# Soft mixture of experts on one core: operand products of two experts moved ahead of the first expert's products, and ScalarE's copies moved ahead of its casts

## The chip, the cores and the metric

The kernel runs on one core of a Trainium2 chip. The metric is the device time of one execution in microseconds (us). TensorE (PE in the profile) multiplies matrices and writes to PSUM; VectorE (DVE) and ScalarE (ACT) do elementwise work and copy results out of PSUM; GpSimd (POOL) and SyncE (SP) mostly issue transfers here. Each engine works through its own list of instructions in order, and the lists are tied together by semaphores.

## The reference

```python
logits_max = np.max(router_logits, axis=-1, keepdims=True)
probs = np.exp(router_logits - logits_max)
probs = probs / np.sum(probs, axis=-1, keepdims=True)
output = np.zeros((batch, seq, expert_hidden), dtype=np.float32)
for e in range(n_experts):
    expert_out = np.matmul(x, expert_weights[e])
    output += probs[:, :, e:e+1] * expert_out
```

Sixteen batches of 512 tokens make 8192 rows of x with 512 values each. There are 8 experts, each with a matrix of 512 by 2048. Every token gets the sum of all eight products, weighted by the softmax of its router logits. All inputs and the output are float32.

## The kernel before

The weighted sum over experts is one large product: the token's x, scaled by each expert's weight, against the stacked expert matrices. The kernel casts to float16, cuts rows, experts and columns into halves and builds the product from seven block products in place of eight, with sums and differences of blocks made by DVE. Nearly all of the run is a list of "stages" that a planner in Python (`run`, `slack`, `later`) lays out slot by slot; from `ordered[0] = True` on, instructions keep the order in which the program writes them.

The change is in the opening stage before that (lines 270 to 336). It computes, for the first 512 rows of x and the first half of the columns, the contribution of the first four experts, without the seven-product scheme, while inputs are still being loaded:

- `cast_block` lets POOL issue the transfers that load and cast the expert weights, one piece for each expert and column half (`b11`); expert 0 of the first half comes in two parts. The x rows (`xs0`) are loaded on the same queue, the first two pieces ahead of all weights.
- `softmax` on a small set of logits gives the weights `ph0[0]` of the first 512 rows. `diag_e(e)` is one DVE instruction (line 112) that makes four diagonal matrices from them, one for each of the four row blocks `j`.
- `early_z0(e, d, js)` makes expert e's left operand: for each row block four small products of x with a diagonal (`ps<-h,w`, 128x128), which transpose and scale x at once, into one PSUM bank. These are called operand products here. `evacuate` casts the bank into `z0[j]`: DVE for even `j`, ACT for odd `j` (lines 238 and 236).
- The loop over `n` (column half) and `e` (expert) then does 16 products for each expert (`ps<-w,z`, 128x512), into four banks. Expert 0 of the first half goes by `QUARTERS`, so that its first eight products need only the first part of its weights, and of these the four for `j` = 0 and 1 come first.
- In the first half, `ahead` puts the operand products of the experts to come between these: expert 1's after eight of expert 0's products, expert 2's after expert 0's sixteen, expert 3's after expert 1's.
- At the first half's expert 2 the program also writes the softmax of further logits: `early_p(1)` for the next 512 rows, with four more diagonals, and `softmax_of_all`, for all rows. The latter's DVE chain (lines 182 to 187 and 112) and ACT exponential (line 184) end in two ACT casts (lines 294 and 295) and four SP stores to `p_dram`, from which later stages read their weights.
- At the end of each half, ACT copies the four banks (line 335) and SP stores them to `kept`.
- In the second half, `early_xp1` makes operands for the first stage of the main list: products with the identity and with ones (`ps<-ident,w`, `ps<-h,ones`) in banks that the first half has freed.

There are eight PSUM banks; a product that writes to a bank waits until the bank's former content has been cast or copied. `mm` (line 132) writes every product of PE, `tt` (line 112) every two-operand instruction of DVE, and `sp` and `pool` (lines 123 and 126) the transfers of their queues, so these lines stand for many places in the code. Instructions on DVE and ACT that go through `dve` and `act` stay in program order.

Of the kernel before, what the change touches and what calls it, by code (L numbers as in the profile page):

```python
# [31 lines left out]
def kernel(  # L32
# [7 lines left out]
    nc = tc.nc  # L40
    P = 128
# [6 lines left out]
    E, _, EH = expert_weights.shape  # L48
# [7 lines left out]
    NHQ = T // HQ  # L56
# [17 lines left out]
    def h_tile(shape, dtype):  # L74
        return hpool.tile(shape, dtype, name="h", tag="h")

    def half():
        return h_tile([P, NB], f32)
# [10 lines left out]
    with tc.tile_pool(name="psum0", bufs=1, space=bass.MemoryType.PSUM) as psum0:  # L89
        zero = wpool.tile([P, NB], f16, name="zero", tag="w")  # L90
# [9 lines left out]
    def note(i):  # L100
        last[i.ins.engine] = i.ins
        if ordered[0]:
            tc.keep_in_program_order(i)
# [5 lines left out]
    act = dve  # L109

    def tt(o, a, b, op):
        dve(nc.vector.tensor_tensor(out=o, in0=a, in1=b, op=op))  # L112
# [9 lines left out]
    def sp(o, i):  # L122
        note(nc.sync.dma_start(out=o, in_=i))
# [4 lines left out]
    def bank():  # L128
        return psum.tile([P, NB], f32, name="ps", tag="ps")

    def mm(ps, z, w, start, stop):
        note(nc.tensor.matmul(ps, z, w, start=start, stop=stop, skip_group_check=True))  # L132
# [3 lines left out]
    def new_w():  # L136
        return wpool.tile([P, K8, NB], f16, name="w", tag="w")
# [31 lines left out]
    def inner_sums(b, t7=None):  # L169

        w = {1: b[0, 0], 2: b[1, 0], 3: b[1, 1], 7: t7 or b[0, 1]}

        def step(p, x, y):
            if p not in w:
                w[p] = new_w()
            tt(w[p], x, y, SUB)
        return w, {5: lambda: step(5, b[0, 1], b[0, 0]), 6: lambda: step(6, b[1, 1], w[5]),
                   4: lambda: step(4, b[1, 0], w[6]), 7: lambda: step(7, b[1, 1], b[0, 1])}

    def softmax(lg, J, pf):  # L180
        mx = h_tile([P, J], f32)
        dve(nc.vector.tensor_reduce(out=mx, in_=lg, axis=AX, op=mybir.AluOpType.max))  # L182
        tt(lg, lg, mx.unsqueeze(2).to_broadcast([P, J, E]), SUB)
        nc.scalar.activation(out=lg, in_=lg, func=mybir.ActivationFunctionType.Exp)  # L184
        sm = h_tile([P, J], f32)
        dve(nc.vector.tensor_reduce(out=sm, in_=lg, axis=AX, op=ADD))  # L186
        dve(nc.vector.reciprocal(out=sm, in_=sm))  # L187
        n = pf.shape[1]
        tt(pf, lg.rearrange("p j e -> p e j")[:, 0:n], sm.unsqueeze(1).to_broadcast([P, n, J]), MUL)
        return pf  # L190
# [27 lines left out]
    def early_p(t):  # L218
        if t == 0:
            return softmax(lg0[t], 4, cpool.tile([P, HE, 4], f16, name="ph0"))  # L220
        pf = softmax(lg0[t], 4, cpool.tile([P, HE, 4], f32, name="pf0"))
        odd = pf.rearrange("p e (q j) -> p e q j", j=2)[:, :, :, 1]
        tt(odd[:, 0:2], odd[:, 0:2], odd[:, 2:4], ADD)
        ph = cpool.tile([P, HE, 4], f16, name="ph1")
        dve(nc.vector.tensor_copy(ph, pf))
        return ph

    def diag(p):

        d = h_tile([P, 4, P], f16)  # L230
        tt(d, ident.unsqueeze(1).to_broadcast([P, 4, P]), p.to_broadcast([P, 4, P]), MUL)
        return d

    def evacuate(o, ps, i):
        if i % 2:
            act(nc.scalar.copy(o, ps))
        else:
            dve(nc.vector.tensor_copy(o, ps))  # L238
# [4 lines left out]
    def diag_e(e):  # L243
        return diag(ph0[0][:, e].unsqueeze(2))

    def early_z0(e, d, js=range(4)):
        for j in js:
            ps = bank()
            for c in range(C):
                mm(ps[:, ds(c * P, P)], xs0[:, j, ds(c * P, P)], d[:, j], c == 0, c == C - 1)  # L250
            evacuate(z0[j][:, e], ps.rearrange("p (c t) -> p c t", c=C), j)
# [5 lines left out]
    def diag_j(j):  # L257
        return diag(ph0[1][:, :, ds(j % 4, 1)])

    def early_xp1(j, d):  # L260
        t, rows = j // 2 - 2, ds(j % 2 * P, P)
        ps = bank()
        for c in range(C):
            mm(ps[:, ds(c * P, P)], xs0[:, j, ds(c * P, P)], ident, c == 0, c == C - 1)
        evacuate(xp1[t][0][:, :, rows], ps.rearrange("p (c t) -> p c t", c=C), 0)
        ps = bank()
        mm(ps, ones, d.rearrange("p e t -> p (e t)"), True, True)
        evacuate(xp1[t][1][:, :, rows], ps.rearrange("p (e t) -> p e t", e=HE), 1)

    R = 4  # L270
    J = HQ // R
    p_dram = dram.tile([NHQ, 3 * HE, HQ], f16, name="p_dram")
# [3 lines left out]
    def load_logits():  # L276
        dve(nc.vector.memset(lg_all[:, 0, 0:1], 0.0))
        dve(nc.vector.memset(lg0[1][:, 0, 0:1], 0.0))
        for q in range(2):
            sp(lg0[1][:, ds(2 * q, 2), :], lg_f[ds((4 + 2 * q) * HQ, HQ)].rearrange("(j p) e -> p j e", p=P))  # L280
        for r in range(R):
            sp(lg_all[ds(r * NHQ, NHQ)], lg_v[r])

    def softmax_of_all():

        pf = softmax(lg_all, J, h_tile([P, E, J], f32))
        pq = h_tile([P, HE, J], f32)
        tt(pq, pf[:, 0:HE], pf[:, HE:E], ADD)
        low = ds(P // 2, P // 2)
        pv = pf.rearrange("p (s e) j -> p s e j", s=2)[low]  # L290
        tt(pv[:, :, 0:2], pv[:, :, 0:2], pv[:, :, 2:4], ADD)
        tt(pq[low, 0:2], pq[low, 0:2], pq[low, 2:4], ADD)
        ph = h_tile([P, 3 * HE, J], f16)
        act(nc.scalar.copy(ph[:, 0:E], pf))  # L294
        act(nc.scalar.copy(ph[:, E:], pq))
        for r in range(R):
            sp(p_dram[:, :, ds(r * J, J)], ph[ds(r * NHQ, NHQ)])

    kept = [dram.tile([2, HQ, NB], f32, name=f"kept_{i}") for i in range(NI)]

# [2 lines left out]
    ORDERS = [(c, j) for c in range(C) for j in range(4)], QUARTERS  # L303

    ds_ = [diag_e(0)]
    for h in range(2):
        early_z0(0, ds_[0], (2 * h, 2 * h + 1))
        for i in range(3 - 2 * h):
            mm(bank(), zero[:, 0:P], zero, True, True)
    load_logits()  # L310
    ds_ += [diag_e(1), diag_e(2)]
    for n in range(2):
        ps = [bank() for _ in range(4)]
        for e in range(HE):
            if n == 0 and e == 1:
                ds_.append(diag_e(3))
            if n == 0 and e == 2:
                ph0.append(early_p(1))
                ds_ = [diag_j(j) for j in range(4, 8)]
                softmax_of_all()  # L320
                w, sums = inner_sums(b11, new_w())
            for c, j in ORDERS[n == 0 and e == 0]:
                mm(ps[j], z0[j][:, e, c], b11[e // 2, n][:, e % 2 * C + c, :],
                   e + c == 0, e == HE - 1 and c == C - 1)
                ahead = {(0, 1, 3): 1, (0, 3, 3): 2, (1, 3, 3): 3}.get((e, c, j))
                if n == 0 and ahead:
                    early_z0(ahead, ds_[ahead])
            if n == 1:
                for j in ((4, 5), (6, 7), (), ())[e]:
                    early_xp1(j, ds_[j - 4])  # L330
                if e == 1:
                    sums[5]()
        for j in range(4):
            o = half()
            act(nc.scalar.copy(o, ps[j]))  # L335
            sp(kept[j // 2][n].rearrange("(p j) m -> j p m", j=2)[j % 2], o)

    ordered[0] = True
    SLOT = 1.73
# [932 lines left out]
```

## Time and profile before

| What | Value |
| --- | --- |
| median of 3 runs | 1371.24 us |
| lowest and highest | 1371.21 and 1373.33 us |
| the profiled execution | 1371.77 us |
| its span, first to last instruction | 1369.9 us |
| PE busy | 1360.8 us (99%) |
| DVE busy | 1122.1 us (82%) |
| ACT busy | 194.7 us (14%) |
| POOL busy | 407.3 us (30%) |
| transfers | 353.79 MB, mean 258 GB/s |

In rows of a timeline the first number is the start and the second the length, in us from the start of the span; then come engine, line, operation, what is written and read, and how many instructions the row merges. What stands in brackets is how long the engine was idle before, and what ended that. The end of a row of products is modelled: the last product's full length lies beyond the start of the next row. In the list of waits the numbers are us in total, times, and the longest one. In rows on transfers `POOLq` or `SPq` names the queue; the last number is the median time from issue to landing.

### The profile page before, as it was taken

Reading aid. Unit: us, or ns where it says so; the run is one execution under the profiler, and the core shown is the slowest. Engines: PE = TensorE matmul, PEld = TensorE weight load, DVE = VectorE, ACT = ScalarE, POOL = GpSimd, SP = SyncE. Lnnn points to the kernel's source line nnn. Section 1 sums busy time; section 2 is a strip of 40 time slices with the busy share of each in tenths; the row PEclk is TensorE's granted clock in tenths of the full one; section 3 lists DMA queues with packets and bytes.
Section 4 is the critical chain, followed back from the end, with each engine's and each line's share of the span. In section 5 each row is a group of like instructions: output and inputs, shape, how many; then the busy total and the mean of one; then the engine's idle time right before and its main releaser. Section 6 shows DMA issues by size and latency. Waiting matters only on the chain.

```text
span 1369.9 us, 18108 instructions
## 1 busy us (share of the span) xinstructions
PE 1360.8 (99%) x6634; PEld 645.9 (47%) x6634; DVE 1122.1 (82%) x1359; ACT 194.7 (14%) x358; POOL 407.3 (30%) x644
## 2 busy tenths in 40 slices
PE   8999999999999999999999999999999999999998
PEld 4455544454444444444444444444444444456554
DVE  5875867789889888788887888888889797898873
ACT  3232211100001111111111100000000000123221
POOL 3123324231223232333323122232332422223232
PEclk9999999999999999999999999999999999999999
DMA  9999999999897999999999978988798979989996
GB/s 181 205 239 230 249 241 280 289 289 367 265 327 231 335 327 306 256 286 310 306 271 343 339 257 222 210 240 203 228 256 222 247 203 291 306 205 239 208 204 119
DMA packets 191945, 353.79 MB, mean 258 GB/s; under 512 B 52976, under 2 KB 87024, under 8 KB 186736
## 3 DMA queue, kind: packets, MB, share of 16 engines
q0 software_dynamic: 88048, 183.02, 56.3%
q1 hardware_dynamic: 98048, 129.63, 31.0%
q10 hardware_dynamic: 5760, 39.99, 7.9%
q8 instruction: 52, 0.85, 0.3%
q14 instruction: 37, 0.30, 0.1%
HBM read 211.85 MB, written 167.97 MB: 277 GB/s over the span
## 4 chain that ended last, share of the span: by engine, by line
PE 98%; DVE 1%; DMA 1%; ACT 0%; issue 0%; POOL 0%; DVEq 0%; POOLq 0%
PE ps L132 98%; DMA w<-in_expert_weights_dram 1%; DVE h L112 0%; POOL w L126 0%; DVE z L112 0%; DVE z L238 0%; DVE h L186 0%; DVE h L187 0%; DVE h L182 0%; ACT h L184 0%; ACT h L294 0%; ACT h L335 0%; ACT h L1209 0%; DVE pf L112 0%; DVE ps L112 0%
## 5 line engine op out<-in xcount | busy, mean ns | idle before, releaser
L132 PE MATMUL ps<-w,z 128*128 128x512 f16 x5256 | 1131.2, 375 | 2.4 <-DMA w<-in_expert_weights_dram 2.4
L132 PEld LDWEIGHTS <-z 128*128 128x128 f16 x5336 | 521.9, 98 | 604.1 <-DVE h L112 2.7
L126 POOL DMA_DIRECT2D out_dram<-h x380 | 249.3, 663 | 746.2 <-ACT h L578 364.4
L112 DVE TENSOR_TENSOR h<-ps,h 128x512 f32<-128x512 f32 x415 | 284.5, 688 | 187.7 <-PE ps L132 169.8
L112 DVE TENSOR_TENSOR z<-xT,pT 128x2048 f16<-128x2048 f16 x216 | 262.2, 1217 | 6.6 <-DMA xT<-w 4.8
L132 PE MATMUL ps<-w,d 128*128 128x512 f16 x880 | 199.1, 379 | 0.0
L132 PEld LDWEIGHTS <-d 128*128 128x128 f16 x880 | 86.1, 98 | 101.7
L112 DVE TENSOR_TENSOR z<-z,d 128x2048 f16<-128x2048 f16 x110 | 131.5, 1217 | 0.0
L578 ACT COPY h<-ps 128x512 f32<-128x512 f32 x64 | 37.5, 586 | 503.7 <-PE ps L132 499.2
L112 DVE TENSOR_TENSOR w<-w 128x1024 f16<-128x1024 f16 (+2 forms) x88 | 99.9, 1146 | 1.8 <-PE ps L132 1.0
L567 ACT COPY h<-ps 128x512 f32<-128x512 f32 x90 | 52.7, 586 | 309.2 <-PE ps L132 297.1
L112 DVE TENSOR_TENSOR ps<-ps,h 128x512 f32<-128x512 f32 (+1 forms) x106 | 62.2, 591 | 23.8 <-PE ps L132 23.2
L112 DVE TENSOR_TENSOR d<-z 128x1024 f16<-128x1024 f16 x110 | 74.6, 687 | 4.2 <-PE ps L132 2.8
L564 ACT COPY h<-ps 128x512 f32<-128x512 f32 x90 | 51.9, 589 | 142.0 <-PE ps L132 132.4
L126 POOL DMA_DIRECT2D kept<-h x56 | 30.9, 552 | 102.6 <-ACT h L567 74.3
L126 POOL DMA_DIRECT2D w<-in_expert_weights_dram x65 | 48.8, 782 | 20.1 <-DMA wd<-w 8.4
L126 POOL DMA_DIRECT2D wd<-w x78 | 44.3, 593 | 32.9 <-DVE w L112 27.6
L112 DVE TENSOR_TENSOR u<-xT,pT 128x2048 f16<-128x2048 f16 x38 | 46.2, 1217 | 0.0
L112 DVE TENSOR_TENSOR h<-h 128x512 f32<-128x512 f32 (+2 forms) x69 | 45.1, 675 | 0.1
L112 DVE TENSOR_TENSOR z<-z,u 128x2048 f16<-128x2048 f16 x34 | 41.4, 1217 | 0.1
L560 ACT COPY ps<-ps 128x512 f32<-128x512 f32 x45 | 25.6, 570 | 99.6 <-PE ps L132 93.8
L112 DVE TENSOR_TENSOR z<-z 128x2048 f16<-128x2048 f16 x32 | 39.1, 1222 | 0.7
(61 smaller groups left out, 278.7 us busy)
## 6 DMA issues: line engine op xcount, KB each, us to landing
out_dram<-h POOLq DMA_DIRECT2D x380, 256.0 KB, 6.9
pT<-p_dram SPq DMA_DIRECT2D x125, 256.0 KB, 6.8
h<-kept SPq DMA_DIRECT2D x108, 256.0 KB, 7.2
w<-wd ACTq DMA_DIRECT2D x25, 1024.0 KB, 8.9
xT<-x SPq DMA_DIRECT2D x74, 256.0 KB, 6.8
w<-in_expert_weights_dram POOLq DMA_DIRECT2D x35, 512.0 KB, 9.9
wd<-w POOLq DMA_DIRECT2D x64, 256.0 KB, 6.5
h<-out_dram SPq DMA_DIRECT2D x60, 256.0 KB, 5.4
```

The costliest lines, as they stand in the source:

```text
L112: dve(nc.vector.tensor_tensor(out=o, in0=a, in1=b, op=op))
L126: note(nc.gpsimd.dma_start(out=o, in_=i, **how))
L132: note(nc.tensor.matmul(ps, z, w, start=start, stop=stop, skip_group_check=True))
L560: act(nc.scalar.copy(self.banks["b"], x))
L564: act(nc.scalar.copy(o[tn], q if p == 5 else x))
L567: act(nc.scalar.copy(o[TN[p]], b if p == 2 else x))
L578: act(nc.scalar.copy(o[tn], b))
```

## The change

`softmax_of_all` no longer issues the two casts and the four stores to `p_dram` itself; it returns a function `keep` that does, and the loop calls it after the first half's copies and stores have been written. The calls of `early_z0` inside the loop over products are gone. Experts 1 and 2 get their operand products before the loop, each with the next expert's diagonals written ahead of it on DVE, and expert 3 gets them after expert 0's sixteen products. The softmax of the further logits is now written at the first half's expert 1, where it was at expert 2. The diagonals of expert 1 stand between the two parts of expert 0's operand products, and one filler product on zeros after the second part is dropped. Both kernels have the same number of every other instruction.

```diff
@@ softmax_of_all
         ph = h_tile([P, 3 * HE, J], f16)
-        act(nc.scalar.copy(ph[:, 0:E], pf))
-        act(nc.scalar.copy(ph[:, E:], pq))
-        for r in range(R):
-            sp(p_dram[:, :, ds(r * J, J)], ph[ds(r * NHQ, NHQ)])
+
+        def keep():
+            act(nc.scalar.copy(ph[:, 0:E], pf))
+            act(nc.scalar.copy(ph[:, E:], pq))
+            for r in range(R):
+                sp(p_dram[:, :, ds(r * J, J)], ph[ds(r * NHQ, NHQ)])
+        return keep
@@ the opening stage
     ds_ = [diag_e(0)]
-    for h in range(2):
-        early_z0(0, ds_[0], (2 * h, 2 * h + 1))
-        for i in range(3 - 2 * h):
-            mm(bank(), zero[:, 0:P], zero, True, True)
+    early_z0(0, ds_[0], (0, 1))
+    for i in range(3):
+        mm(bank(), zero[:, 0:P], zero, True, True)
+    ds_.append(diag_e(1))
+    early_z0(0, ds_[0], (2, 3))
     load_logits()
-    ds_ += [diag_e(1), diag_e(2)]
+    for e in (1, 2):
+        ds_.append(diag_e(e + 1))
+        early_z0(e, ds_[e])
     for n in range(2):
         ps = [bank() for _ in range(4)]
         for e in range(HE):
             if n == 0 and e == 1:
-                ds_.append(diag_e(3))
-            if n == 0 and e == 2:
+                early_z0(3, ds_[3])
                 ph0.append(early_p(1))
                 ds_ = [diag_j(j) for j in range(4, 8)]
-                softmax_of_all()
+                keep_p = softmax_of_all()
                 w, sums = inner_sums(b11, new_w())
             for c, j in ORDERS[n == 0 and e == 0]:
                 mm(ps[j], z0[j][:, e, c], b11[e // 2, n][:, e % 2 * C + c, :],
                    e + c == 0, e == HE - 1 and c == C - 1)
-                ahead = {(0, 1, 3): 1, (0, 3, 3): 2, (1, 3, 3): 3}.get((e, c, j))
-                if n == 0 and ahead:
-                    early_z0(ahead, ds_[ahead])
@@ the end of a half
             act(nc.scalar.copy(o, ps[j]))
             sp(kept[j // 2][n].rearrange("(p j) m -> j p m", j=2)[j % 2], o)
+        if n == 0:
+            keep_p()
```

## The prediction, made before the run

> **What bounds the kernel now.** The page comes first: how much of the span TensorE (PE) is busy, and which engine the chain that ended last runs on.
>
> ```profile
> span 1369.9 us, 18108 instructions
> ...
> PE 1360.8 (99%) x6634; PEld 645.9 (47%) x6634; DVE 1122.1 (82%) x1359; ACT 194.7 (14%) x358; POOL 407.3 (30%) x644
> ...
> PE 98%; DVE 1%; DMA 1%; ACT 0%; issue 0%; POOL 0%; DVEq 0%; POOLq 0%
> ```
>
> PE is the bound for 98% of the chain. An edit gains only if it removes PE work or closes one of PE's gaps. The view of waits for PE lists them all:
>
> ```profile
> PE ps L132 <- DMA w<-in_expert_weights_dram: 2.4, 1, 2.4
> PE ps L132 <- ACT h L335: 1.4, 1, 1.4
> ...
> PE ps L132 <- DVE ps L112: 0.2, 1, 0.2
> ```
>
> The two large ones lie in the opening stage, which is the stage that is changed. The timeline of PE places them:
>
> ```profile
> 7.08 0.62 PE L132 MATMUL ps<-h,w 128*128 128x128 f16 x8
> 7.53 0.38 PE L132 MATMUL ps<-zero 128*128 128x512 f16 x1
> 10.28 1.89 PE L132 MATMUL ps<-w,z 128*128 128x512 f16 x8 [2.37 <-DMA w<-in_expert_weights_dram]
> 12.01 1.06 PE L132 MATMUL ps<-h,w 128*128 128x128 f16 x16
> 12.90 1.89 PE L132 MATMUL ps<-w,z 128*128 128x512 f16 x8
> 14.62 1.06 PE L132 MATMUL ps<-h,w 128*128 128x128 f16 x16
> 15.52 3.62 PE L132 MATMUL ps<-w,z 128*128 128x512 f16 x16
> 18.97 1.06 PE L132 MATMUL ps<-h,w 128*128 128x128 f16 x16
> 19.86 10.52 PE L132 MATMUL ps<-w,z 128*128 128x512 f16 x48
> 31.76 0.38 PE L132 MATMUL ps<-ident,w 128*128 128x128 f16 x4 [1.37 <-ACT h L335]
> 37.04 13.98 PE L132 MATMUL ps<-w,z 128*128 128x512 f16 x64
> 50.85 3.62 PE L132 MATMUL ps<-w,d 128*128 128x512 f16 x16
> ```
>
> Rows `ps<-h,w` build left operands ("operand products", one group of 16 for each expert), rows `ps<-w,z` multiply them by weights. Starts give the true pace: 64 weight products from 37.04 to 50.85 are 0.216 us each, and a group of 16 operand products costs 12.90 - 12.01 = 0.89 or 15.52 - 14.62 = 0.90 us. Gap one: PE has nothing before expert 0's weights at 10.28. Gap two: 48 products from 19.86 would be issued by 19.86 + 48 x 0.216 = 30.23, yet the next work starts at 31.76, so 1.53 us pass (the row's 1.37 counts from the modelled end). The chain shows why:
>
> ```profile
> 30.21 0.62 ACT h L294
> 30.82 0.31 ACT h L295
> 31.13 0.49 ACT h L335
> ...
> 31.76 1183.47 PE ps L132 x5620
> ```
>
> ScalarE (ACT) first casts the routing weights (L294, L295), which waited for VectorE's (DVE) softmax, and only then copies the first half's result (L335) that frees a PSUM bank. After 31.76 the chain is PE alone for 1183 us, so time won before it should reach the end.
>
> **The change, part by part.** *1. Operand products ahead.* The groups of experts 1 and 2 move into gap one; expert 3's group goes behind expert 0's sixteen products. Nothing is removed but one filler product on zeros (row 7.53, inside the gap: 0 us). The cover is the gap, and the groups need DVE's diagonals in time:
>
> ```profile
> 7.51 0.69 DVE L238 CAST z<-ps 128x512 f16<-128x512 f32 x1 [0.70 <-PE ps L132]
> 8.13 0.69 DVE L112 TENSOR_TENSOR h<-ident,ph 128x512 f16<-128x512 f16 x1
> 20.60 0.18 DVE L182 TENSOR_REDUCE h<-lg 128x4 f32<-128x32 f32 x1
> ...
> 26.21 0.63 ACT L184 ACTIVATE h<-h 128x512 f32<-128x512 f32 x1 [4.94 <-DVE h L112]
> 31.04 2.04 ACT L335 COPY h<-ps 128x512 f32<-128x512 f32 x4
> 43.50 2.05 ACT L335 COPY h<-ps 128x512 f32<-128x512 f32 x4 [5.62 <-PE ps L132]
> ...
> 31.16 2.71 SPq L123 DMA_DIRECT2D p_dram<-h  x4
> 45.95 1.24 SPq L123 DMA_DIRECT2D pT<-p_dram  x2
> ```
>
> Expert 1's diagonal now stands before the cast at 7.51; the row's idle 0.70 us holds its 0.69, so its group runs from about 7.5 to 8.4. Expert 2's diagonal stays at 8.13 and ends at 8.82; its group runs from about 8.9 to 9.8, done before 10.28. Expert 0's products start at 10.28 as before, since the weights decide. They write banks that the casts of the moved groups must free: the fifth product, at 11.1, needs DVE's cast of expert 1, which behind two ops of 0.69 ends near 9.5; the sixth needs ACT's first cast of expert 2, near 10.1. Neither binds. From 10.28 PE then runs without the two groups in its way: 0.89 + 0.90 = **1.79 us earlier** at the end of the first half, if the weights keep up.
>
> *What is late next: weights.* POOL's later issues are each released by the landing of an earlier piece, and so tell when it landed, to 0.3 us:
>
> ```profile
> 11.73 0.76 POOL L126 DMA_DIRECT2D w<-in_expert_weights_dram  x1 [0.57 <-DMA w<-in_expert_weights_dram]
> 14.47 0.74 POOL L126 DMA_DIRECT2D w<-in_expert_weights_dram  x1 [1.98 <-DMA w<-in_expert_weights_dram]
> 17.59 0.70 POOL L126 DMA_DIRECT2D w<-in_x_dram  x1 [2.38 <-DMA w<-in_expert_weights_dram]
> 21.09 0.71 POOL L126 DMA_DIRECT2D w<-in_x_dram  x1 [2.80 <-DMA w<-in_expert_weights_dram]
> ...
> 25.83 0.72 POOL L126 DMA_DIRECT2D w<-in_x_dram  x1 [1.83 <-DMA w<-in_expert_weights_dram]
> ...
> w<-in_expert_weights_dram POOLq DMA_DIRECT2D x1, 512.0 KB, 18.9
> ...
> w<-in_expert_weights_dram POOLq DMA_DIRECT2D x1, 512.0 KB, 18.7
> ...
> w<-in_x_dram POOLq DMA_DIRECT2D x1, 256.0 KB, 12.7
> ```
>
> The first four rows end the waits for expert 0's second part, expert 1, 2 and 3 of the first half. Landings are thus at most 11.7, 14.5, 17.6 and 21.1. New needs: expert 0's second part at 10.28 + 8 x 0.216 = 12.01; expert 1 at 13.74 + 0.89 (expert 3's group) = 14.63; expert 2 at 18.09; expert 3 at 21.55. Every piece is in time, by 0.2 to 0.5 us on these upper bounds. I take no wait; the other end of this bound is 0.5 us lost. The first half ends at 25.01, where it ended at 26.8.
>
> *2. ACT copies first.* The copies (2.04 us) now follow the first half's last products: about 24.6 to 26.6. The exponential (26.21) stands ahead of them, and DVE's softmax chain moves with expert 3's casts, which now follow a group that starts at 13.74 instead of 18.97: 20.60 becomes about 15.4, the exponential about 21.0. So it doesn't hold the copies. The second half's first expert runs from 25.01 to 28.47, and PE then takes the banks, free since 26.6: gap two closes, **1.53 us**. The bounds are 1.37 (the row) and 1.53; I take the starts. Were the exponential as late as now, the copies would end at 28.9 and the first bank still come free at 27.3, so the cover holds even then.
>
> *3. What is moved.* The two casts (0.93 us on ACT) now start after the copies at 26.6, with DVE's weights ready near 25, and end near 27.5; behind them on ACT stand the pT casts, first needed near 29. Hidden. On the SP queue the four stores of the half now stand ahead of the four p_dram stores; these still go out near 27.6 to 30.3, ahead of the 31.16 shown, and their readers (45.95, then about 42.6) wait behind the second half's stores anyway. DVE's stores and sums behind the second half only move with PE. Cost 0; without the cover it would be 0.93.
>
> *4. Contention.* What the SP queue sends:
>
> ```profile
> kept<-h SPq DMA_DIRECT2D x8, 256.0 KB, 4.1
> ...
> p_dram<-h SPq DMA_DIRECT2D x4, 48.0 KB, 6.5
> ```
>
> The half's stores now run from about 25.2 beside weights that are still loading. The second half's experts 2 and 3 land at 11.73 + 18.9 = 30.6 and 14.47 + 18.7 = 33.2 and are needed at 28.47 + 0.87 + 3.46 + 0.87 = 33.67 and 37.13: 3.0 and 3.9 us to spare. In the trace the last x pieces went beside the same eight stores: four of 256 KB between 33.2 and 25.83 + 12.7 = 38.5, 1.33 us each, against half of a weight piece's 33.2 - 30.6 = 2.6. So sharing costs under 0.1 us a piece; I take 0.
>
> **Sum.** 1.79 + 1.53 = 3.3 us. The profiled execution took 1371.77 us for a span of 1369.9; this gives 1368.5. It is 0.5 above the median of 1371.24, so the median should be 1367.9, 0.24% less.
>
> **Rivals.** *A. Weights become the bound.* Slack falls to a few tenths in part 1. If the pieces land 2 us later beside busier engines, the 1.79 is gone and the copy half stays: 1371.2 - 1.5 = 1369.7. Against it: nothing in the order of POOL's issues ahead of these pieces changes.
>
> *B. The queues share by turns.* Suppose that the software queue with the weights gets half the engines as long as stores are waiting. Stores and p_dram are 4 x 256 + 4 x 48 KB, 1.25 MB. Expert 2's piece of the second half, 30.6 - 25.2 = 5.4 us of transfer away when they start, would take 10.8 and land at 36.0: a wait of 2.4 us, net gain 0.9, time 1370.3. The 1.33 us a piece speaks against half shares.
> The Trainium skill, DMA: Bandwidth & Descriptors (Queues, rings and completion order), states that each DMA engine goes round-robin between queues, a packet at a time; by that rule alone B's 1370.3 stands, and the 1.33 us of this trace doesn't bear it out.
>
> *C. The shift is lost later*, to some transfer whose time doesn't move with PE: 1371.2. The view of waits shows none that PE meets after 31.76, against it.
>
> *D. Slower: the stores starve the weights.* If the SP queue were served first, the last weights (33.2) could be held back by the 4.1 us that a store takes now until it lands and the 6.5 us of p_dram: 43.8 against a need at 37.13, a wait of 6.7, net +3.4: 1374.6. It turns slower once these weights come after 37.1 + 3.3 = 40.4. The same 1.33 us speaks against it.
>
> **Numbers.** Forecast 0.68; A 0.10, B 0.08, C 0.06, D 0.08. 0.2% is 2.7 us, about what a measurement of this kernel can tell. The forecast's own range is 1367.0 to 1368.9 (0.5 for weights, 0.16 for gap two, 0.4 for the runs), nine tenths of it beyond 0.2%: faster 0.63. A, B, C and the forecast's rest make same 0.28; D and a little of C slower 0.09. The range over cases, without D and C: 1366.9 to 1370.3.
>
> **What the new profile would show.** PE's groups of 16 operand products from 7.5 to 9.8 and at 13.74; no PE wait on ACT L337 (the copies' new line); the first `ps<-w,d` at 47.5 instead of 50.85; PE's wait for weights about 0.5 instead of 2.4; p_dram issued near 27.6. New PE waits on weights between 14 and 38 us would make A or B right; a start of `ps<-w,d` at 47.5 with an unchanged end, C.

## The result and the profile after

| What | Before | After |
| --- | --- | --- |
| median of the runs made side by side | 1371.57 us (8 runs, 1371.21 to 1373.63) | 1367.59 us (8 runs, 1367.38 to 1368.08) |
| the profiled execution | 1371.77 us | 1367.46 us |
| its span | 1369.9 us | 1365.7 us |

The ratio is 0.9971, with a 95% interval from 0.9962 to 0.9981. The kernel became faster by 0.29%, or 4.0 us between medians; 1367.9 was forecast.

The page of the changed kernel: span, busy time, and the chain that ended last.

```profile
span 1365.7 us, 18104 instructions
...
PE 1360.4 (100%) x6633; PEld 646.0 (47%) x6633; DVE 1121.4 (82%) x1359; ACT 194.7 (14%) x358; POOL 407.3 (30%) x644
...
PE 99%; DVE 0%; ACT 0%; issue 0%
```

PE's busy time is what it was (1360.8 before, less one filler product), and the span is 4.2 us shorter: only gaps went. The complete list of PE's waits in the changed kernel:

```profile
PE every L94 <- DVE zero L91: 1.3, 1, 1.3
PE ps L132 <- DVE h L112: 0.2, 1, 0.2
```

The waits of 2.4 us for weights and 1.4 us for ACT are gone, and no wait took their place. The timeline of PE in the changed kernel, opening stage:

```profile
6.89 1.73 PE L132 MATMUL ps<-h,w 128*128 128x128 f16 x24
8.79 1.07 PE L132 MATMUL ps<-h,w 128*128 128x128 f16 x16 [0.17 <-DVE h L112]
9.84 3.63 PE L132 MATMUL ps<-w,z 128*128 128x512 f16 x16
13.31 1.06 PE L132 MATMUL ps<-h,w 128*128 128x128 f16 x16
14.20 13.98 PE L132 MATMUL ps<-w,z 128*128 128x512 f16 x64
28.01 0.39 PE L132 MATMUL ps<-ident,w 128*128 128x128 f16 x4
...
33.22 13.98 PE L132 MATMUL ps<-w,z 128*128 128x512 f16 x64
47.04 3.62 PE L132 MATMUL ps<-w,d 128*128 128x512 f16 x16
```

The groups of experts 1 and 2 fill the time up to 9.84, and `ident` at 28.01 follows its 64 products with no wait in brackets. The first `ps<-w,d` comes at 47.04 instead of 50.85, 3.81 us earlier. Of this, 0.44 us is the start of expert 0's products at 9.84 instead of 10.28, because its weights happened to land sooner; the change does not touch that transfer. The other 3.37 us are the change, against 3.32 in the forecast.

ACT's timeline in the changed kernel shows the copies (L337) ahead of the casts (L296, L297), and the SP queue's timeline shows the stores in the new order:

```profile
20.54 0.63 ACT L184 ACTIVATE h<-h 128x512 f32<-128x512 f32 x1 [4.94 <-DVE h L112]
24.11 2.05 ACT L337 COPY h<-ps 128x512 f32<-128x512 f32 x4 [2.94 <-PE ps L132]
26.02 0.65 ACT L296 CAST h<-h 128x512 f16<-128x512 f32 x1
```

```profile
24.72 1.85 SPq L123 DMA_DIRECT2D kept<-h  x4
27.00 4.61 SPq L123 DMA_DIRECT2D p_dram<-h  x4
```

After the opening the two kernels' work runs in step, 3.8 to 3.9 us apart, for more than 1150 us. Then a short wait comes in the kernel before that the list of the changed kernel doesn't have. The timeline of PE there, before and then after:

```profile
1215.05 1.89 PE L132 MATMUL ps<-w,z 128*128 128x512 f16 x8
1217.11 1.03 PE L132 MATMUL ps<-t,s 128*128 128x256 f16 x8 [0.17 <-DVE ps L112]
```

```profile
1211.13 1.89 PE L132 MATMUL ps<-w,z 128*128 128x512 f16 x8
1212.86 1.04 PE L132 MATMUL ps<-t,s 128*128 128x256 f16 x8
```

The two kernels stand 1215.05 - 1211.13 = 3.92 us apart ahead of the wait and 1217.11 - 1212.86 = 4.25 behind it. Of the runs below, the profiles of the copies alone, of the products alone and of one of the two runs with the gap filled have this wait too; the other run with the gap filled and the one without fillers do not, though they too are the old order. None of the six profiles of kernels with both edits has it in full (the one with doubled stores loses 0.2 us there). Whether the change has a part in it isn't shown. So 3.37 (the change) + 0.44 (an earlier landing) + 0.33 (this wait) + 0.11 (small steps on the way, not traced) = 4.25 us is the difference of the two spans, 4.2.

### The profile page after: what moved, and what is told of

Same layout as the page of the kernel before. It is cut to its first block, busy times and chain, and to the rows that moved or that the text cites. A ratio compares the mean times of both kernels' runs of the same rounds, so it can differ in the third digit from the quotient of the medians.

```text
span 1365.7 us, 18104 instructions
## 1 busy us (share of the span) xinstructions
PE 1360.4 (100%) x6633; PEld 646.0 (47%) x6633; DVE 1121.4 (82%) x1359; ACT 194.7 (14%) x358; POOL 407.3 (30%) x644
## 3 DMA queue, kind: packets, MB, share of 16 engines
q1 hardware_dynamic: 98048, 129.63, 31.3%
## 4 chain that ended last, share of the span: by engine, by line
PE 99%; DVE 0%; ACT 0%; issue 0%
PE ps L132 99%; PE every L94 0%; DVE z L238 0%; DVE h L112 0%; ACT h L1213 0%; DVE zero L91 0%; DVE tiny L86 0%
## 5 line engine op out<-in xcount | busy, mean ns | idle before, releaser
L112 DVE TENSOR_TENSOR z<-xT,pT 128x2048 f16<-128x2048 f16 x216 | 262.2, 1217 | 7.8 <-DMA xT<-w 7.5
L112 DVE TENSOR_TENSOR z<-z,d 128x2048 f16<-128x2048 f16 x110 | 131.5, 1217 | 0.0
L126 POOL DMA_DIRECT2D kept<-h x56 | 30.9, 553 | 104.3 <-ACT h L571 73.6
L112 DVE TENSOR_TENSOR u<-xT,pT 128x2048 f16<-128x2048 f16 x38 | 46.2, 1217 | 0.0
```

The source lines that it names most:

```text
L126: note(nc.gpsimd.dma_start(out=o, in_=i, **how))
```

## The experiments

The theory was that the two edits close two separate gaps, 1.79 us by the operand products and 1.53 us by ACT's new order. The main rival was that the operand products alone close both, because they also move the softmax on DVE. Two more questions stood beside this: what the stores cost the weights they now run beside, and why some executions of the kernel before take 1373 us rather than 1371. Each time below is a median beside runs of the kernel before on the same chip.

### The products alone, and the copies alone

The first kernel is the changed one with casts and `p_dram` stores back ahead of the copies. The second is the kernel before, with ACT's copies first and nothing else.

```diff
products_only, against the changed kernel
-                keep_p = softmax_of_all()
+                softmax_of_all()()
...
-        if n == 0:
-            keep_p()
```

```diff
copies_only, against the kernel before
-        act(nc.scalar.copy(ph[:, 0:E], pf))
-        act(nc.scalar.copy(ph[:, E:], pq))
-        for r in range(R):
-            sp(p_dram[:, :, ds(r * J, J)], ph[ds(r * NHQ, NHQ)])
+
+        def keep():
...
+        return keep
...
-                softmax_of_all()
+                keep_p = softmax_of_all()
...
+        if n == 0:
+            keep_p()
```

> Only the operand products are moved; the casts and p_dram stores stand ahead of the copies as in the kernel before. Theory of the prediction, that the two parts add up: PE still waits about 1.5 us for the copies near 28 us, time about 1369.3. Rival: with the products moved, DVE's softmax chain follows expert 3's group and ends near 24.7 us in the changed kernel's trace, so the casts are over by 25.6, the copies by 27.7, and PE asks for the first bank at 28.0: no wait, time like the changed kernel's, 1367.6. After that trace I hold with the rival.

> Only ACT's order is changed; the operand products stay where they are in the kernel before. Theory: PE's wait for the copies (1.53 us by the starts) goes, since the exponential is over at 26.8 and the first copy at 27.4, and PE asks for the bank at 30.2; the wait of 2.4 for expert 0's weights stays; time 1371.5 - 1.5 = 1370.0. Rival: something else late (the weights of the softmax, the exponential) takes the wait's place, and the time stays at 1371.5.

Products alone: 1367.87 us (7 runs), ratio 0.9974 (0.9963 to 0.9985). Copies alone: 1369.89 us (10 runs), ratio 0.9987 (0.9978 to 0.9997). The kernel before beside both was at 1371.48. So the first edit gives 3.6 us and the second, alone, 1.6; together they give 4.0, not 5.2. The rival was right: gap two closes by either edit. ACT's timeline of the kernel with the products alone shows why:

```profile
25.75 0.62 ACT L296 CAST h<-h 128x512 f16<-128x512 f32 x1 [3.37 <-DVE h L112]
...
26.58 2.04 ACT L337 COPY h<-ps 128x512 f32<-128x512 f32 x4
```

and PE's timeline of the same kernel:

```profile
11.05 3.63 PE L132 MATMUL ps<-w,z 128*128 128x512 f16 x16 [1.52 <-DMA w<-in_expert_weights_dram]
...
29.29 0.39 PE L132 MATMUL ps<-ident,w 128*128 128x128 f16 x4
```

The casts still stand ahead of the copies, but they start at 25.75, where the kernel before had 30.21: DVE's softmax moved forward with expert 3's operand products. The first copy ends a quarter of 2.04 us after 26.58, near 27.1, and PE asks for that bank at 29.29. So there are 2.2 us to spare without ACT's new order. This profiled execution took 1369.24, the slowest of its seven; its 1.52 us wait shows the weights landing late, at about 11.0 rather than 9.8. What the second edit adds on top of the first is 0.3 us by the medians of two separate comparisons, which do not tell that from nothing.

### How many groups belong ahead

One kernel moves only expert 1's group into the gap, the other moves expert 3's too.

```diff
one_ahead, against the changed kernel
-    for e in (1, 2):
-        ds_.append(diag_e(e + 1))
-        early_z0(e, ds_[e])
+    ds_.append(diag_e(2))
+    early_z0(1, ds_[1])
+    ds_.append(diag_e(3))
...
+                early_z0(2, ds_[2])
                 early_z0(3, ds_[3])
```

```diff
three_ahead, against the changed kernel
-    for e in (1, 2):
-        ds_.append(diag_e(e + 1))
+    for e in (1, 2, 3):
+        if e < 3:
+            ds_.append(diag_e(e + 1))
         early_z0(e, ds_[e])
...
-                early_z0(3, ds_[3])
```

> As the changed kernel, but only expert 1's group of operand products stands ahead of expert 0's products; expert 2's group stands behind them with expert 3's. Theory: each group in the gap is worth its 0.89 us, so the first ps<-w,d starts 0.9 later than in the changed kernel, 47.9, and the time is 1368.5. Rival: the weights of experts 1 to 3 are the bound after 10 us, and one group more or less on PE changes nothing: 47.0 and 1367.6.

> As the changed kernel, but expert 3's group too stands ahead of expert 0's products. Theory: the gap is full; the third group waits for its diagonal, which DVE ends near 10.5, and runs to 11.4, so expert 0's products start 1.7 us later than the weights would let them (11.5 for 9.8), and 0.89 is saved further on: 0.8 slower than the changed kernel, 1368.4. Rival: every group moved is worth 0.9, time 1366.7.

One ahead took 1368.85 us (ratio 0.9979, 0.9970 to 0.9989), 1.26 us above the changed kernel's 1367.59; a group's 0.9 us had been expected, and in its profiled execution 0.34 us more is a later landing of the first weights (products from 10.18, not 9.84). Three ahead took 1368.37 (0.9972, 0.9962 to 0.9982), 0.8 above. PE's timelines, first of one ahead, then of three ahead:

```profile
10.18 3.63 PE L132 MATMUL ps<-w,z 128*128 128x512 f16 x16 [1.27 <-DMA w<-in_expert_weights_dram]
```

```profile
10.79 1.07 PE L132 MATMUL ps<-h,w 128*128 128x128 f16 x16 [0.73 <-DVE h L112]
11.69 17.43 PE L132 MATMUL ps<-w,z 128*128 128x512 f16 x80
```

With one group 1.27 us of the gap stay open. With three the gap is overfilled: expert 3's diagonal is not there until 10.79, and expert 0's products start at 11.69 although their weights had landed. Two groups fit. Both sides fit a term of about 0.9 us for each group, to within the few tenths that the landing of the first weights moves.

### What the stores cost the weights

The forecast took it that a piece of weights loses under 0.1 us beside the stores. The view of transfers, taken of one POOL issue at a time, gives each issue's time to landing; the timeline of POOL gives the start of the issue. In the changed kernel, for the second half's experts 2 and 3, the timeline and then the view of transfers:

```profile
11.37 0.76 POOL L126 DMA_DIRECT2D w<-in_expert_weights_dram  x1 [0.56 <-DMA w<-in_expert_weights_dram]
...
14.17 0.74 POOL L126 DMA_DIRECT2D w<-in_expert_weights_dram  x1 [2.05 <-DMA w<-in_expert_weights_dram]
```

```profile
w<-in_expert_weights_dram POOLq DMA_DIRECT2D x1, 512.0 KB, 19.5
...
w<-in_expert_weights_dram POOLq DMA_DIRECT2D x1, 512.0 KB, 21.1
```

They land at 11.37 + 19.5 = 30.9 and 14.17 + 21.1 = 35.3, so the second takes 4.4 us after the first, where it took 2.6 before. To test that it is the stores, one kernel issues the first half's four stores behind the second half's, and another issues each of the four twice, the second time to a spare tensor.

```diff
stores_late, against the changed kernel
-                sp(p_dram[:, :, ds(r * J, J)], ph[ds(r * NHQ, NHQ)])
+                dve(nc.sync.dma_start(out=p_dram[:, :, ds(r * J, J)], in_=ph[ds(r * NHQ, NHQ)]))
...
-            sp(kept[j // 2][n].rearrange("(p j) m -> j p m", j=2)[j % 2], o)
+            held_o.append((kept[j // 2][n].rearrange("(p j) m -> j p m", j=2)[j % 2], o))
+        if n == 1:
+            for to, o in held_o[4:] + held_o[:4]:
+                dve(nc.sync.dma_start(out=to, in_=o))
```

```diff
stores_twice, against the changed kernel
+    spare = [dram.tile([P, NB], f32, name=f"spare_{j}") for j in range(4)]
...
             sp(kept[j // 2][n].rearrange("(p j) m -> j p m", j=2)[j % 2], o)
+            if n == 0:
+                sp(spare[j], o)
```

> As the changed kernel, but the first half's four stores to kept are issued behind the second half's. Theory: these stores slow the last weights (expert 3 of the second half landed at 35.25 us in the changed kernel, 4.4 us behind expert 2's piece, for 2.54 in the kernel before); without them it lands near 33, 2.6 to 2.8 behind. Rival: the small p_dram packets slow it, and it still lands after 34.5. The time is that of the changed kernel, 1367.6, by both, since PE asks for this piece at 36.7.

> As the changed kernel, but each of the first half's four stores is issued a second time, to a spare place in DRAM: 1 MB more beside the last weights. Theory (the queues share): expert 3's piece of the second half lands 1.5 to 2.5 us later than the 35.25 us of the changed kernel, 36.8 to 37.8, PE, which asks for it at 36.7, waits 0.1 to 1.1 us on weights, and the time is 1367.7 to 1368.7. Rival (the stores take no share of the weights' queue): landing near 35.3, no wait, 1367.6.

The same two views of the kernel with late stores:

```profile
11.31 0.76 POOL L126 DMA_DIRECT2D w<-in_expert_weights_dram  x1 [0.57 <-DMA w<-in_expert_weights_dram]
...
14.10 0.74 POOL L126 DMA_DIRECT2D w<-in_expert_weights_dram  x1 [2.03 <-DMA w<-in_expert_weights_dram]
```

```profile
w<-in_expert_weights_dram POOLq DMA_DIRECT2D x1, 512.0 KB, 18.3
...
w<-in_expert_weights_dram POOLq DMA_DIRECT2D x1, 512.0 KB, 18.2
```

and of the kernel with the stores doubled:

```profile
11.79 0.76 POOL L126 DMA_DIRECT2D w<-in_expert_weights_dram  x1 [0.56 <-DMA w<-in_expert_weights_dram]
...
14.58 0.74 POOL L126 DMA_DIRECT2D w<-in_expert_weights_dram  x1 [2.04 <-DMA w<-in_expert_weights_dram]
```

```profile
w<-in_expert_weights_dram POOLq DMA_DIRECT2D x1, 512.0 KB, 19.5
...
w<-in_expert_weights_dram POOLq DMA_DIRECT2D x1, 512.0 KB, 21.9
```

Without stores beside them the pieces land at 29.6 and 32.3, 2.7 us apart; with four stores at 30.9 and 35.3, 4.4 apart; with eight at 31.3 and 36.5, 5.2 apart. So the stores do slow the weights: four of 256 KB put off the last piece by 35.3 - 32.3 = 3.0 us. In the changed kernel that is still hidden, because PE asks for this piece at 33.22 + 16 x 0.216 = 36.7; 1.4 us are left, not the forecast's 3.9.

The doubled stores took 1369.12 us (10 runs, 1367.87 to 1372.21; ratio 0.9985, 0.9976 to 0.9994). The expectation had that piece land at 36.8 to 37.8 and PE wait for it. The profiled execution, 1368.26, has no wait for that piece, which lands 0.6 us before its need; what the slower ones wait for isn't shown.

The late stores took 1374.2 us (10 runs, ratio 1.0016, 1.0007 to 1.0026), where 1367.6 had been expected: right on the weights, wrong by 6.6 us on the time. Its list of waits for PE names a place that the forecast never looked at:

```profile
PE ps L132 <- DVE h L112: 2.2, 2, 1.9
PE ps L132 <- DVE t L112: 1.5, 1, 1.5
```

DVE is late there, and its own timeline says what it waited for. First the late stores, then the changed kernel:

```profile
70.06 1.23 DVE L112 TENSOR_TENSOR z<-xT,pT 128x2048 f16<-128x2048 f16 x1 [5.42 <-DMA xT<-w]
77.54 1.23 DVE L112 TENSOR_TENSOR z<-xT,pT 128x2048 f16<-128x2048 f16 x1 [6.25 <-DMA xT<-w]
```

```profile
73.38 1.23 DVE L112 TENSOR_TENSOR z<-xT,pT 128x2048 f16<-128x2048 f16 x1 [7.54 <-DMA xT<-w]
```

The SP queue carries the stores, then loads, then transposes (`xT<-w`). Four more stores at its head put off the second set of transposes from 52.75 to 55.42. The first of that set then took 9.2 us from issue to landing in place of 5.3. The likely reason is that it now meets two 512 KB weight loads that POOL issues from 55.56 on; that was not tried by itself. DVE gets the last transpose 77.54 - 73.38 = 4.2 us later, which its slack no longer covers. In the kernel with doubled stores the same set starts at 54.35, and PE has a short wait at the same place. PE's rows there, first with late stores, then with doubled stores, then in the changed kernel:

```profile
90.74 5.28 PE L132 MATMUL ps<-w,z 128*128 128x512 f16 x16 [1.93 <-DVE h L112]
```

```profile
87.56 2.76 PE L132 MATMUL ps<-w,z 128*128 128x512 f16 x16 [0.20 <-DVE h L112]
```

```profile
86.77 2.76 PE L132 MATMUL ps<-w,z 128*128 128x512 f16 x16
```

In this profile of the changed kernel DVE's sum that frees the bank starts at 85.84 and ends 0.68 us later, at 86.52, only 0.25 us before PE takes the bank. In the kernel before it was 3.0 us (87.61 and 90.58), and in a second profile of the changed kernel 2.3 (84.52 and 86.81). The change brought PE forward by 3.8 us here, and the transposes that DVE waits for by 1.1 us in one profile and 3.1 in the other (74.47 before, 73.38 and 71.37 after). With late stores PE's row comes 90.74 - 86.77 = 4.0 us later; most of the rest of the 6.6 us is the clock. Windows of PE in the kernel with late stores (start and end, length, busy time and products, granted clock, share of the DMA engines, GB/s):

```profile
88.00:91.00 3.00, 0.86 (x5) 0.71 1.44 169
91.00:96.00 5.00, 5.00 (x17) 0.50 0.96 375
```

After two waits near each other, of 1.5 and 1.9 us, the granted clock was 0.50 for 5 us, and 16 products took 5.28 us instead of 2.76.

### The clock after the gap

The executions of the kernel before spread widely upwards. The theory was that the gap before expert 0's weights sometimes lowers the granted clock. One kernel fills the gap with ten products on zeros, which are meant to hold the clock and change nothing else; it was run twice. Another drops the kernel's four fillers, so that PE idles earlier and, for the same landing of the weights, longer. The changed kernel was run again beside them.

```diff
before_filled and before_filled_2, against the kernel before
-        for i in range(3 - 2 * h):
-            mm(bank(), zero[:, 0:P], zero, True, True)
+        if h == 0:
+            for i in range(3):
+                mm(bank(), zero[:, 0:P], zero, True, True)
+        else:
+            filled = bank()
+            for i in range(10):
+                mm(filled, zero[:, 0:P], zero, True, True)
```

```diff
no_fillers, against the kernel before
-        for i in range(3 - 2 * h):
-            mm(bank(), zero[:, 0:P], zero, True, True)
```

> The kernel before, with ten filler products on zeros in one bank, in place of one, after expert 0's operand products: PE is busy through gap one and waits no longer than 0.5 us there, and nothing else changes. Theory: some executions of the kernel before lose their clock for a while after the gap (the profile of copies_only, which has the same gap, shows a granted clock of 0.50 from 12 to 14.4 us and 1371.89 us where its median is 1369.89); with the gap filled the executions above 1372.5 us, 6 of 26, go, and the lowest stay near 1371. Rival: the two groups of executions have another cause, and a fifth of these too lie above 1372.5.

> The changed kernel once more, beside the three above: how far its first weights' landing (9.80 us), its wait at that place and its time (1367.59) move from one profile to another. Theory: the landing moves by some tenths and the first products with it; the 0.44 us that the kernel before lost near 1216 us (a wait for DVE) are no part of the change and may or may not come back.

> The kernel before without its four filler products in the opening stage: PE is idle for 0.65 us more between expert 0's two parts, and from 7.5 us to the first weights. Theory (the gap can cost PE its clock): more executions run their first products at half clock, as in the profile of copies_only, and at least four in ten lie 1.5 to 2.5 us above the lowest, near 1373. Rival (the slower executions have another cause, later in the run): as many as in the kernel before, about one in five, and the profile shows a granted clock of 1.00 from 10 to 20 us.

> Before_filled again, for more executions: 1 of its 11 lay above 1372.5 us, 13 of 64 of the kernel before. Theory (the gap costs the clock): again at most one in ten above 1372.5, and the lowest near 1370.6. Rival: one in five.

Windows of PE between 7 and 14.4 us (columns as above): the kernel before, then the one without fillers, then the one with the gap filled.

```profile
12.00:14.40 2.40, 2.40 (x24) 1.00 1.33 230
```

```profile
12.00:14.40 2.40, 2.40 (x20) 0.56 1.34 233
```

```profile
7.00:10.00 3.00, 3.00 (x21) 1.00 1.12 179
...
12.00:14.40 2.40, 2.40 (x24) 1.00 1.32 228
```

In the profiled execution of the kernel before the clock stayed at 1.00 after a gap of 2.37 us; without fillers the mean of this window fell to 0.56 after a gap of 2.48 us, only 0.11 longer. The kernel with only ACT's copies first, whose profiled execution took 1371.89 where most of its runs took 1369.2 to 1370.0, shows it too, after 2.63 us. Its timeline of PE, and then its window of PE:

```profile
10.24 2.46 PE L132 MATMUL ps<-w,z 128*128 128x512 f16 x8 [2.63 <-DMA w<-in_expert_weights_dram]
12.49 1.91 PE L132 MATMUL ps<-h,w 128*128 128x128 f16 x16
14.20 2.20 PE L132 MATMUL ps<-w,z 128*128 128x512 f16 x8
```

```profile
12.00:14.40 2.40, 2.40 (x19) 0.50 1.34 230
```

Its group of operand products took 14.20 - 12.49 = 1.7 us instead of 0.9, and `ident` stood at 31.84, where the kernel before has 31.76: the 1.5 us that it won at gap two had been lost here. Over all executions the counts agree. Each run lists its mean clock over the span; of 77 executions of the kernel before in these three comparisons, 18 took over 1372.5 us, and 15 of the 18 list a clock of 0.999 or less, against 7 of the 59 others. Without fillers it was 10 of 11 executions, and the one at 1.000 took 1370.37, the least of them. The times alone do not separate this kernel from the kernel before (median 1372.45 against 1371.50, ratio 1.0001 with 0.9992 to 1.0010): 8 of the 21 executions beside it list 0.999 or less too. With the gap filled it was 3 of 22, none of them above 1371.7; two of the 22 took over 1372.5, but these list 1.000, so something else than the clock can make a run long too. Where an execution without a trace lost its clock isn't shown, and 0.999 alone is a weak sign: the profiles of the products alone and of the changed kernel's second series list it, with 1.00 in every window of 20 us up to 1360.

The medians with the gap filled are 1371.41 (ratio 1.0001, 0.9992 to 1.0010) and 1371.27 (0.9997, 0.9988 to 1.0006): the filling wins nothing in the usual execution, and none of its 22 was long with a low clock, against 15 of 77. The changed kernel fills the gap with useful products. Its second series took 1367.72 (7 runs, 1367.36 to 1368.49; ratio 0.9972, 0.9962 to 0.9983), and the 15 executions of both series stay below 1368.5. So a part of the 4.0 us between medians may be that the kernel before sometimes loses the clock; its shorter executions, near 1371.2, are some 3.6 us above the changed kernel's.

## Why the prediction was right, and where it was not

*Part 1, operand products ahead (1.79 us): right.* The groups stand at 7.5 to 9.7, PE waits for nothing when weights land at 9.8, and the later pieces were in time, though closer than forecast. By the same upper bounds expert 1's piece had landed by 14.17 and PE took it at 14.20, and expert 2's by 17.61, with PE at 14.20 + 16 x 0.216 = 17.66; the forecast had 0.2 and 0.5 us to spare. The kernels with one and three groups bracket the term.

*Part 2, ACT copies first (1.53 us): right in size, wrong in what closes the gap.* The forecast worked out that DVE's softmax moves from 20.60 to 15.4 (measured 14.94) and used this only to show that the exponential does not hold the copies. The same shift brings the casts forward from 30.21 to 25.75, and this alone closes gap two, as the kernel with the products alone shows. The sum of 3.3 us stands, because the gap closes once; but the 1.53 us were credited to the edit that, on top of the first, adds 0.3 us by the medians, which these runs do not tell from nothing.

*Part 3, moved casts and `p_dram` stores: hidden, as forecast.* The casts start at 26.02 and the `p_dram` stores go out from 27.00, against 27.6 forecast.

*Part 4, contention ("under 0.1 us a piece"): wrong.* The trace of before showed x pieces beside stores, 1.33 us each, and that price was carried over to weights. But only four of the eight stores were issued by then (33.96 to 36.73; the rest from 44.11), and in the kernel with late stores, where no store of the half runs beside them, the same x pieces land 1.4 us apart (33.7 to 38.0). So the 1.33 held no price of sharing; why the stores slow weights and not these x pieces stays open. The measured loss is 3.0 us over two pieces. It stayed hidden under the slack that the same paragraph had worked out, 3.9 us, of which 1.4 is left: the term was 0 because of that slack, not because of the price that the forecast gave.

*Sum and time.* Forecast 3.3 us and 1367.9; the opening gave 3.37 and the median was 1367.59. The two profiled spans differ by 0.9 us more than forecast, mostly by the landing of the first weights (0.44) and the wait for DVE near 1217 us (0.33). That the time came out within 0.3 us is in part luck: the forecast started from a median of three runs, 1371.24, and the eight beside the changed kernel have 1371.57, from which the same sum gives about 1368.2. "PE alone for 1183 us" was true only up to the wait near 1217.

*The rivals.* A (weights become the bound) did not occur: no wait for weights is listed. C (the shift is lost later) did not occur either; the shift is 3.81 us at 47 us and is kept. Its mechanism is real, though: the transposes near 73 us did not move with PE, and only 0.25 us of the 3.0 us to spare near 87 us was left in one of two profiles. The list of waits, on which the forecast ruled C out, shows no such margins. D (stores starve the weights) had its mechanism too strong: the last piece came at 35.3, not 43.8. B (shares by turns) lies between: it put expert 2's piece 5.4 us later, and the piece came 30.9 - 29.6 = 1.3 us later than without stores. The Trainium skill, DMA: Bandwidth & Descriptors (Queues, rings and completion order), has each engine alternate between queues by packets. Some such sharing is now seen, which the forecast had denied on the 1.33 us a piece, but at a price well under half shares.

## What to carry to other kernels

When a block of work is moved, follow everything queued behind it on the other engines: here the move of some products closed a second gap by bringing a softmax chain forward, and an edit made for that gap was left with nothing to close. A hidden transfer is worth its slack in microseconds, so state the slack at the need (1.4 us here) and test it by doubling the load. A list of waits shows where an engine is late, not where it is nearly late: check the whole queue behind a moved transfer, since four stores put later on one queue cost 6.6 us some 40 us downstream, where the changed kernel had 0.25 us to spare.

## What the runs showed of the hardware that was not expected

- After a gap of 2.48 us on PE (no fillers) and of 2.63 us (copies alone) the granted clock fell to 0.50 and was back at 1.00 some 3 to 4 us later; after 2.37 us (before) it stayed at 1.00 in the one profile. Two waits of 1.5 and 1.9 us near each other (late stores) brought it to 0.50 for 5 us. The Trainium skill, TensorE: Matmul & The Clock Gate (Part 1: The HAM clock gate), gives about 3.4 us of idling and calls its window free-running; that some executions are hit and others not agrees, the length does not.
- The first 256 KB of weights, issued at 2.89 or 2.90 us in every kernel, took 6.9 us to land in the changed kernel's profile, 7.3 in that of before and 8.1 in that of the products alone. Over all twelve profiles it was 6.4 to 7.3 in the kernels that leave the operand products in their place and 6.8 to 8.1 in those that move them, so the earlier landing in the changed kernel's profile is no effect of the change. The first products of every kernel here wait for this load or start close to its landing, and carry this spread.
